# Raising the priority of the linear layers' matmuls, five of every six, in a three-block f32 model

## The chip, the cores and the metric

The kernel runs on one core of a Trainium2 chip. The metric is the device time of one execution in microseconds (us), and lower is better. Before the change it is 3328.61 us, the median of three runs (3328.02 to 3330.11).

## The reference

An activation of 512 tokens by 1024 channels passes through three residual blocks, all in float32. Each block projects its input with one wide matrix, feeds slices of the result to sequence mixers, projects the mixers' outputs, gates and sums them, and ends in a gated feed-forward network. The blocks differ in their mixers: a short convolution, pooling, a 31-tap convolution and differential attention in the first; a gated delta rule and an RWKV-7 scan in the second; gated linear attention and a state-space scan in the third. Of the second block, where most of what follows plays, the reference is:

```python
h = rms_norm_2(x, norm1_w[i]) * (1.0 + scale1) + shift1
p = h @ w_in[i]
qkv_a, z_a, b_a, a_a, p_b, gl_a, gl_b = split_cols(p, IN_SIZES)
y_a = gated_deltanet(qkv_a, z_a, b_a, a_a, conv_gdn[i], a_log[i], dt_bias[i], onorm_gdn[i])
y_b = rwkv7_time_mix(p_b, mu_rwkv[i], w0[i], w2[i], a0[i], a2[i], g2[i], k_k[i], k_a[i],
                     r_k[i], lnx_w[i], lnx_b[i])
y_a = y_a.astype(x.dtype) @ w_branch_gdn[i]
y_b = y_b.astype(x.dtype) @ w_branch_rwkv[i]
merged = jax.nn.sigmoid(gl_a) * y_a + jax.nn.sigmoid(gl_b) * y_b
x = x + gate1 * (merged @ w_out[i])
```

## The kernel before

Activations lie with channels on the 128 partitions and tokens along the free axis, so a 512 x 1024 activation is eight tiles of 128 x 512. Every linear layer keeps float32 precision by splitting both operands into a high part (float32r) and a remainder. One 128 x 128 weight block is then three matmuls over 512 tokens: high weight times high input, high weight times low input, low weight times high input. `lin` (line 358) makes one column of 128 output channels: it walks over the 8 (or 4, 11, 16) weight blocks along the contraction and accumulates 24 (or 12, 33, 48) matmuls into one PSUM bank of the pool `mm` (three banks). These are lines 368, 369 and 370. `product` (line 350, matmuls at lines 354 to 356) does the same on weights that were taken beforehand, for half columns and for the context of the third block. `tokens` (lines 404 to 406) is a third form, with the roles of weight and activation swapped.

Weights stream from HBM in pieces of eight blocks (`load`, line 315): one DMA, a copy on ScalarE that makes the high part (line 324) and a subtraction on VectorE that makes the low part (line 325).

The mixers issue many small matmuls of their own: transposes (line 655), block inversions (lines 707 and 714, inside `invert`), 64-row score blocks (line 1370), sums over the partitions in two halves (lines 616 and 617), state-space products (lines 2068 and 2082) and so on. Below they are called the mixers' matmuls, and those of lines 354 to 356, 368 to 370 and 404 to 406 the linear matmuls.

In the second block the mixers work head pair by head pair, j = 0 to 3. For each, `lins(j)` (line 1203) makes seven linear columns, then `rwkv` (line 1299, tiles tagged r, ra and fr) and `gdn` (line 1453, tiles tagged g, ga and fg) run side by side as generators, and their results are normalised and stored. `lins(j + 1)` and some gate columns (`aside`, 2, 1, 1 and 12 of them) follow in the text. After j = 3 the branch projection `w_branch_rwkv_2` reads the mixers' outputs, `yr`: its first three parts were stored earlier and are reloaded, its fourth is the last head pair's own result Y.

No order is written by hand. A scheduler takes the instructions as written, with their dependencies, and places on each engine, whenever that engine is free in its own estimate, the ready instruction of the highest priority; earlier in the text means higher priority. `first(n)` (line 252) raises what is inside by n places, 4000 by default, which is used on the weight pieces and on copies out of PSUM. The order that comes out is fixed in the program: at run time each engine issues its queue in order and waits at an instruction whose operands are not there yet. Linear columns written later than a mixer step thus serve as fill: they take the gaps while the mixer waits for VectorE or ScalarE.

Of the kernel before, what the change touches and what calls it, by code (L numbers as in the profile page):

```python
# [2 lines left out]

# [182 lines left out]
class K:  # L186
# [158 lines left out]
    def column(self, out, x):  # L345

        for a in range(0, P, 32):
            self.T.matmul(out[a:a + 32], lhsT=x[:, a:a + 32], rhs=self.ones[:, 0:1], start=True, stop=True)

    def product(self, ps, w, x, n=slice(0, S)):  # L350

        last = len(w) - 1
        for k, (wh, wl) in enumerate(w):
            self.T.matmul(ps[:, n], lhsT=wh, rhs=x[0][k][:, n], start=k == 0, stop=False)  # L354
            self.T.matmul(ps[:, n], lhsT=wh, rhs=x[1][k][:, n], start=False, stop=False)  # L355
            self.T.matmul(ps[:, n], lhsT=wl, rhs=x[0][k][:, n], start=False, stop=k == last)  # L356

    def lin(self, x, name, col, row=0, xc=None, n=S):

        self.tick()  # L360
        out = self.bank("mm")[:, :n]
        outc = self.bank("mm")[:, :256] if xc else None
        if xc is None:
            for k in range(len(x[0])):
                w = self.take([(name, row + P * k, col)])
                self.ahead()
                (wh, wl), last = w[0], len(x[0]) - 1
                self.T.matmul(out, lhsT=wh, rhs=x[0][k], start=k == 0, stop=False)  # L368
                self.T.matmul(out, lhsT=wh, rhs=x[1][k], start=False, stop=False)  # L369
                self.T.matmul(out, lhsT=wl, rhs=x[0][k], start=False, stop=k == last)  # L370
            return out
        w = self.take([(name, row + P * k, col) for k in range(len(x[0]))])
        self.product(outc, w, xc, slice(0, 256))
        self.product(out, w, x)
        self.ahead()
        return out, outc
# [1742 lines left out]
```

## Time and profile before

| | before |
|---|---|
| median of three runs | 3328.61 us |
| the profiled execution's own time | 3330.9 us |
| its span, first to last instruction | 3329.1 us |
| mean granted TensorE clock | 0.992 of full |
| TensorE (PE) busy | 3242.3 us, 97% |
| VectorE (DVE) busy | 2234.4 us, 67% |
| ScalarE (ACT) busy | 1497.2 us, 45% |
| the largest group of linear matmuls, line 368 on inputs h, 128 x 512 | 2400 recorded, 395 ns each as modelled |

Busy times are shares of the span. Matmuls are pipelined and the profile models their ends, so two that follow each other overlap in the records; what a matmul costs is read from one start to the next. An "x" after a row of the timeline counts merged records; a full-float32 matmul of the mixers leaves two records, a transpose one for each 128 x 128 block. In brackets stands the idle time of the engine ahead of the row, and what ended it.

### The profile page before, as it was taken

To read this page: it belongs to the slowest core of one execution; us is meant where nothing else is said; L and a number is where in the kernel's file an instruction comes from. 1 tells how busy PE (TensorE), PEld (TensorE's weight loads), DVE (VectorE), ACT (ScalarE), POOL (GpSimd) and SP (SyncE) were. 2 spreads that over 40 slices of the span, in tenths; PEclk is the share of its full clock that TensorE was granted. 3 is DMA by queue.
4 is the path that set the end of the run, shared out by engine and by line. 5 is a ranking of instruction groups with operands and counts; after the bars stand their busy time and mean duration, and the time that the engine had idled before them with its cause. 6 is when DMAs were issued, how large, how long until landed. Compare 5 with 4: busy or idle time off the path is not lost.

```text
span 3329.1 us, 48326 instructions
## 1 busy us (share of the span) xinstructions
PE 3242.3 (97%) x19041; PEld 2700.3 (81%) x19041; DVE 2234.4 (67%) x3675; ACT 1497.2 (45%) x2491; POOL 101.0 (3%) x186
## 2 busy tenths in 40 slices
PE   7999999999999999999999999999999999999998
PEld 6778888888887887887888887888877778888887
DVE  5696645986578577566887567777687996363344
ACT  6443433432346656654332334645546665232222
POOL 0000000000000000000000000000000001000000
PEclk9999999999999999999999999999999999999999
DMA  4223333665332112125367324222227567423332
GB/s 134 64 70 98 95 117 102 215 202 161 107 103 76 46 50 73 58 64 171 122 203 242 95 81 133 69 78 92 81 80 239 171 208 239 131 88 101 95 95 76
DMA packets 128324, 393.33 MB, mean 118 GB/s; under 512 B 16056, under 2 KB 23480, under 8 KB 128096
## 3 DMA queue, kind: packets, MB, share of 16 engines
q1 hardware_dynamic: 113776, 346.82, 33.6%
q0 software_dynamic: 13168, 42.36, 3.7%
q8 instruction: 150, 2.46, 0.3%
q10 hardware_dynamic: 1152, 1.05, 0.1%
q14 instruction: 78, 0.64, 0.1%
HBM read 358.44 MB, written 31.74 MB: 117 GB/s over the span
## 4 chain that ended last, share of the span: by engine, by line
PE 88%; DVE 6%; ACT 4%; issue 2%; DMA 1%; SPq 0%; POOL 0%; DVEq 0%; ACTq 0%; POOLq 0%
PE mm L368 20%; PE mm L369 20%; PE mm L370 20%; PE mm L354 3%; PE mm L355 3%; PE mm L356 3%; PE s L2082 1%; DVE wl L325 1%; PE s L2068 1%; ACT wh L324 1%; PE r L1370 1%; PE g L655 1%; PE mm L405 1%; PE r L655 1%; PE mm L406 1%
## 5 line engine op out<-in xcount | busy, mean ns | idle before, releaser
L368 PE MATMUL mm<-h,wh 128*128 128x512 f32 x2400 | 947.6, 395 | 1.8 <-ACT t L948 1.5
L369 PE MATMUL mm<-h,wh 128*128 128x512 f32 x2400 | 948.5, 395 | 0.0
L370 PE MATMUL mm<-h,wl 128*128 128x512 f32 x2400 | 947.3, 395 | 0.0
L324 ACT ACTIVATE wh<-wr 128x1024 fp32r<-128x1024 f32 x464 | 491.4, 1061 | 949.8 <-PE mm L369 663.5
L325 DVE TENSOR_TENSOR wl<-wr,wh 128x1024 fp32r<-128x1024 f32 x464 | 567.2, 1224 | 467.6 <-ACT wh L324 462.2
L368 PEld LDWEIGHTS mm<-h,wh 128*128 128x128 f32 x2400 | 452.7, 189 | 98.4 <-issue 5.5
L370 PEld LDWEIGHTS mm<-h,wl 128*128 128x128 f32 x2400 | 452.7, 189 | 96.9 <-issue 6.0
L369 PEld LDWEIGHTS mm<-h,wh 128*128 128x128 f32 x2400 | 452.8, 189 | 96.2 <-issue 5.4
L368 PE MATMUL mm<-p,wh 128*128 128x512 f32 x599 | 233.6, 390 | 0.0
L369 PE MATMUL mm<-p,wh 128*128 128x512 f32 x599 | 233.4, 390 | 0.1
L370 PE MATMUL mm<-p,wl 128*128 128x512 f32 x599 | 233.1, 389 | 0.0
L354 PE MATMUL mm<-h,wh 128*128 128x256 f32 (+1 forms) x480 | 159.5, 344 | 14.4 <-DVE t L1930 5.3
L355 PE MATMUL mm<-h,wh 128*128 128x256 f32 (+1 forms) x480 | 160.1, 339 | 1.1 <-DVE h L569 1.0
L356 PE MATMUL mm<-h,wl 128*128 128x256 f32 (+1 forms) x480 | 158.6, 335 | 0.0
L301 DVE SCALAR_TENSOR_TENSOR ac<-wa,adas,ac 128x1024 f32<-128x1024 f32 x98 | 125.5, 1282 | 23.9 <-DMA wa<-wa 23.5
L369 PEld LDWEIGHTS mm<-p,wh 128*128 128x128 f32 x599 | 112.4, 188 | 23.9 <-DVE p L430 0.8
L368 PEld LDWEIGHTS mm<-p,wh 128*128 128x128 f32 x599 | 112.4, 188 | 23.5
L370 PEld LDWEIGHTS mm<-p,wl 128*128 128x128 f32 x599 | 112.4, 188 | 23.4
L354 PEld LDWEIGHTS mm<-h,wh 128*128 128x128 f32 x480 | 92.4, 198 | 25.8 <-ACT h L568 4.6
L355 PEld LDWEIGHTS mm<-h,wh 128*128 128x128 f32 x480 | 94.3, 198 | 10.0 <-DVE h L569 2.0
L356 PEld LDWEIGHTS mm<-h,wl 128*128 128x128 f32 x480 | 94.6, 198 | 8.5
L750 DVE SCALAR_TENSOR_TENSOR f<-mm,par,f 128x511 f32<-128x511 f32 (+1 forms) x128 | 95.5, 746 | 1.1
(661 smaller groups left out, 5244.6 us busy)
## 6 DMA issues: line engine op xcount, KB each, us to landing
wr<-w SPq DMA_DIRECT2D x464, 512.0 KB, 3.7
wa<-wa SPq DMA_DIRECT2D x96, 512.0 KB, 4.3
e<-cum SPq DMA_DIRECT2D x64, 256.0 KB, 5.1
x<-x POOLq DMA_DIRECT2D x40, 256.0 KB, 4.5
s<-ecum SPq DMA_DIRECT2D x64, 128.0 KB, 4.8
cd<-t POOLq DMA_DIRECT2D x24, 256.0 KB, 2.3
gt<-t POOLq DMA_DIRECT2D x16, 256.0 KB, 2.5
fr<-gt SPq DMA_DIRECT2D x16, 256.0 KB, 3.0
```

The source lines that it names most:

```text
L301: self.V.scalar_tensor_tensor(a, raw, s[:, k, m:m + 1], a, op0=ALU.mult, op1=ALU.add)
L324: self.A.activation(hi, raw, AF.Copy)
L325: self.V.tensor_tensor(lo, raw, hi.bitcast(F32), op=ALU.subtract)
L354: self.T.matmul(ps[:, n], lhsT=wh, rhs=x[0][k][:, n], start=k == 0, stop=False)
L355: self.T.matmul(ps[:, n], lhsT=wh, rhs=x[1][k][:, n], start=False, stop=False)
L356: self.T.matmul(ps[:, n], lhsT=wl, rhs=x[0][k][:, n], start=False, stop=k == last)
L368: self.T.matmul(out, lhsT=wh, rhs=x[0][k], start=k == 0, stop=False)
L369: self.T.matmul(out, lhsT=wh, rhs=x[1][k], start=False, stop=False)
L370: self.T.matmul(out, lhsT=wl, rhs=x[0][k], start=False, stop=k == last)
L405: self.T.matmul(ps, lhsT=a, rhs=wl, start=False, stop=False)
L655: self.z.T.transpose(ps[:, c * P:(c + 1) * P], src[:, c * P:(c + 1) * P], self.z.ident)
L750: z.V.scalar_tensor_tensor(out[:, d:], src[:, :S - d], w[:, n - 1 - d:n - d], out[:, d:], op0=ALU.mult, op1=ALU.add)
```

## The change

In the two functions `product` and `lin` every matmul but one in six is put inside `self.first()`, so that its priority is 4000 places higher. Left as it was is the first matmul of weight blocks 0, 2, 4 and so on; the two that follow it on the same block, and all three of the next block, are raised. `tokens` is untouched, and so is everything that is computed.

```diff
+    def goes_on(self, k=1):
+
+        return self.first() if k % 2 else nullcontext()
+
     def product(self, ps, w, x, n=slice(0, S)):
 
         last = len(w) - 1
         for k, (wh, wl) in enumerate(w):
-            self.T.matmul(ps[:, n], lhsT=wh, rhs=x[0][k][:, n], start=k == 0, stop=False)
-            self.T.matmul(ps[:, n], lhsT=wh, rhs=x[1][k][:, n], start=False, stop=False)
-            self.T.matmul(ps[:, n], lhsT=wl, rhs=x[0][k][:, n], start=False, stop=k == last)
+            with self.goes_on(k):
+                self.T.matmul(ps[:, n], lhsT=wh, rhs=x[0][k][:, n], start=k == 0, stop=False)
+            with self.goes_on():
+                self.T.matmul(ps[:, n], lhsT=wh, rhs=x[1][k][:, n], start=False, stop=False)
+                self.T.matmul(ps[:, n], lhsT=wl, rhs=x[0][k][:, n], start=False, stop=k == last)
...
-                self.T.matmul(out, lhsT=wh, rhs=x[0][k], start=k == 0, stop=False)
-                self.T.matmul(out, lhsT=wh, rhs=x[1][k], start=False, stop=False)
-                self.T.matmul(out, lhsT=wl, rhs=x[0][k], start=False, stop=k == last)
+                with self.goes_on(k):
+                    self.T.matmul(out, lhsT=wh, rhs=x[0][k], start=k == 0, stop=False)
+                with self.goes_on():
+                    self.T.matmul(out, lhsT=wh, rhs=x[1][k], start=False, stop=False)
+                    self.T.matmul(out, lhsT=wl, rhs=x[0][k], start=False, stop=k == last)
```

In the changed program line numbers are higher by eight below these functions, and the three matmuls of `lin` stand at lines 375, 377 and 378, those of `product` at 359, 361 and 362. Counted over TensorE's whole queue, both programs have 16347 matmuls. The mixers' ones stand in 407 groups between linear matmuls before and in 308 groups after; groups that begin with a transpose at line 655 go from 63 to 33, with line 2082 from 33 to 23, with line 1005 from 21 to 12, with the sums of lines 616 and 617 from 69 to 52.

Three places show what moves. The first is TensorE's queue at the start of the second block's first head pair. The names g1411 and g1459 are banks of the gdn side (g1411 receives the transposed decay rows, line 1201), mm1446 and mm1688 are linear columns. Before:

```order
L368 MATMUL mm1446_8187<-h898_4694,wh1436_8112 128x512
L369 MATMUL mm1446_8187<-h899_4695,wh1436_8112 128x512
L370 MATMUL mm1446_8187<-h898_4694,wl1437_8113 128x512
L368 MATMUL mm1446_8187<-h900_4696,wh1436_8112 128x512
L655 MATMUL g1411_7960<-con2_64,ga1402_7921 128x128 x4
L369 MATMUL mm1446_8187<-h901_4697,wh1436_8112 128x512
```

After, in the changed program:

```order
L375 MATMUL mm1688_9076<-h898_4694,wh1442_8151 128x512
L377 MATMUL mm1688_9076<-h899_4695,wh1442_8151 128x512
L378 MATMUL mm1688_9076<-h898_4694,wl1443_8152 128x512
L663 MATMUL g1411_7960<-con2_64,ga1402_7921 128x128 x4
L624 MATMUL g1459_8236<-ga1457_8234,bd64r4_66 128x512
L625 MATMUL g1459_8236<-ga1458_8235,bd64r4_66 128x512
L375 MATMUL mm1688_9076<-h900_4696,wh1442_8151 128x512
```

The transposes into g1411 stood inside column mm1446, 13 matmuls into it; now they stand in the next column, 12 matmuls into mm1688, which is 23 linear matmuls later.

The second place is TensorE's queue in the last head pair, j = 3, where `rwkv` goes from its bonus sum (bank r2332, lines 616 and 617) to its first scores (bank r2349, line 1370). mm2573 is a gate column; mm2617 and mm2626 are columns of the branch projection behind the mixers. Before, the end of that stretch:

```order
L370 MATMUL mm2573_12806<-h894_4690,wl2566_12742 128x512
L368 MATMUL mm2573_12806<-h896_4692,wh2565_12741 128x512
L369 MATMUL mm2573_12806<-h897_4693,wh2565_12741 128x512
L1370 MATMUL r2349_11872<-ra2296_11681,ra2315_11740 128x128 x4
L1370 MATMUL r2361_11905<-ra2296_11681,ra2315_11740 128x128 x4
L370 MATMUL mm2573_12806<-h896_4692,wl2566_12742 128x512
```

After, the whole of it:

```order
L377 MATMUL mm2626_13029<-fg2598_12951,wh2590_12911 128x512
L378 MATMUL mm2626_13029<-fg2597_12950,wl2591_12912 128x512
L624 MATMUL r2332_11796<-ra2330_11794,bd64r4_66 128x512
L625 MATMUL r2332_11796<-ra2331_11795,bd64r4_66 128x512
L1378 MATMUL r2349_11872<-ra2296_11681,ra2315_11740 128x128
L663 MATMUL g2344_11841<-con2_64,ga2342_11837 128x128 x4
L663 MATMUL g2345_11853<-con2_64,fg2278_11566 128x128 x4
L663 MATMUL g2348_11861<-con2_64,fg2284_11605 128x128 x4
L1378 MATMUL r2349_11872<-ra2296_11681,ra2315_11740 128x128 x3
```

Before, 28 linear matmuls stood between the second half of the sum and the scores; now none does, since all gate columns and what the branch projection can do without Y stand ahead of the sum.

The third place is the end of that head pair: the sums of Y's two normalisations (banks r2523 and r2531) and the branch projection's first matmuls on Y. Before, from the end of the last gate column mm2588:

```order
L616 MATMUL r2531_12520<-ra2529_12518,bd64r4_66 128x512
L370 MATMUL mm2588_12908<-h906_4702,wl2581_12844 128x512
L368 MATMUL mm2617_12989<-fg2594_12944,wh2585_12877 128x512
L617 MATMUL r2531_12520<-ra2530_12519,bd64r4_66 128x512
L369 MATMUL mm2617_12989<-fg2595_12945,wh2585_12877 128x512
L370 MATMUL mm2617_12989<-fg2594_12944,wl2586_12878 128x512
```

After:

```order
L1455 MATMUL r2520_12494<-fr2257_11425,ra2515_12478 128x128 x3
L624 MATMUL r2523_12501<-ra2521_12499,bd64r4_66 128x512
L625 MATMUL r2523_12501<-ra2522_12500,bd64r4_66 128x512
L624 MATMUL r2531_12520<-ra2529_12518,bd64r4_66 128x512
L625 MATMUL r2531_12520<-ra2530_12519,bd64r4_66 128x512
L375 MATMUL mm2617_12989<-ra2602_12960,wh2585_12877 128x512
L377 MATMUL mm2617_12989<-ra2603_12961,wh2585_12877 128x512
```

From the second half of r2332's sum to the first matmul on Y the queue held 143 linear matmuls before and holds 9 after; the other 134 stand ahead of that sum.

## Rows read from the trace of the kernel before

**Rows 1.** The page: the busy time of the engines, and the chain that ended last by engine.

```profile
PE 3242.3 (97%) x19041; PEld 2700.3 (81%) x19041; DVE 2234.4 (67%) x3675; ACT 1497.2 (45%) x2491; POOL 101.0 (3%) x186
...
PE 88%; DVE 6%; ACT 4%; issue 2%; DMA 1%; SPq 0%; POOL 0%; DVEq 0%; ACTq 0%; POOLq 0%
```

**Rows 2.** The timeline of TensorE in a linear column of the second block. The first two rows are five linear matmuls apart; the third is one half of a sum between two linear matmuls. Columns: start, length, engine, line, operation, output and inputs, shape, count.

```profile
1299.95 0.40 PE L368 MATMUL mm<-h,wh 128*128 128x512 f32 x1
...
1301.09 0.39 PE L370 MATMUL mm<-h,wl 128*128 128x512 f32 x1
...
1302.91 0.41 PE L616 MATMUL r<-ra,bd64r 128*128 128x512 f32 x1
1303.16 0.39 PE L369 MATMUL mm<-h,wh 128*128 128x512 f32 x1
```

**Rows 3.** The same view at two other interruptions of linear columns: a pair of transposes in the second block, with a run of five transposes further on, and line 2082 (128 x 64 weights) in the third block, there also in a long run.

```profile
1458.60 0.48 PE L369 MATMUL mm<-h,wh 128*128 128x512 f32 x1
1458.91 0.41 PE L655 MATMUL g<-con,mga 128*128 128x128 f32 x2
1459.08 0.48 PE L370 MATMUL mm<-h,wl 128*128 128x512 f32 x1
1459.39 0.61 PE L707 MATMUL r<-ra,mra 128*128 128x128 f32 x4
...
1471.11 0.71 PE L655 MATMUL g<-con,ga 128*128 128x128 f32 x5
1471.66 0.61 PE L707 MATMUL r<-ra,mra 128*128 128x128 f32 x4
...
2565.70 0.48 PE L370 MATMUL mm<-h,wl 128*128 128x512 f32 x1
2566.11 0.43 PE L2082 MATMUL s<-e,g 128*64 128x128 f32 x2
2566.47 0.50 PE L368 MATMUL mm<-h,wh 128*128 128x512 f32 x1
2566.81 0.39 PE L369 MATMUL mm<-h,wh 128*128 128x512 f32 x1
...
2571.01 1.74 PE L2082 MATMUL s<-e,g 128*64 128x128 f32 x26
2572.68 0.87 PE L2006 MATMUL s<-con,xs 128*128 128x128 f32 x6
```

**Rows 4.** What TensorE waited for from 1000 to 1530 us, the second block's mixers: engine, output, line and releaser, total us, times, longest us.

```profile
PE g L655 <- ACT ga L1198: 3.9, 1, 3.9
PE g L1478 <- DVE fg L1230: 3.2, 3, 1.3
...
PE r L616 <- ACT ra L1289: 2.2, 3, 1.1
```

**Rows 5.** Stretches from 1000 to 1530 us in which the clock was granted at half: the stretch and its length, then busy time and count of PE, PEld, DVE, ACT and POOL, then the granted clock, the DMA share and GB/s.

```profile
1008.90:1012.30 3.40, 3.20 (x10) 2.71 (x11) 3.12 (x5) 2.83 (x6) 0.00 (x0) 0.50 0.75 167
1145.50:1148.80 3.30, 3.30 (x9) 2.62 (x9) 1.42 (x3) 1.17 (x1) 1.08 (x2) 0.50 0.58 209
1159.10:1162.40 3.30, 3.30 (x12) 2.59 (x11) 2.44 (x7) 1.08 (x2) 0.00 (x0) 0.50 0.00 0
1275.20:1278.50 3.30, 3.07 (x9) 1.89 (x7) 3.30 (x5) 3.25 (x5) 0.54 (x1) 0.50 0.05 21
1520.90:1524.30 3.40, 3.40 (x9) 2.67 (x8) 3.21 (x6) 2.04 (x3) 0.00 (x0) 0.50 0.56 183
```

**Rows 6.** TensorE's timeline at the end of one of the waits at line 1478.

```profile
1157.63 1.16 PE L1478 MATMUL g<-fg 64*128 64x128 f32 x8 [1.25 <-DVE fg L1230]
```

**Rows 7.** Five stretches of the last head pair, from the bonus sum to the first matmul on Y, columns as in rows 5.

```profile
1422.60:1429.20 6.60, 6.31 (x29) 4.89 (x27) 6.57 (x12) 3.03 (x6) 0.37 (x1) 1.00 0.08 29
1429.20:1444.70 15.50, 15.48 (x97) 12.63 (x97) 13.51 (x27) 8.54 (x20) 0.71 (x2) 1.00 0.36 118
1444.70:1491.20 46.50, 46.42 (x392) 42.48 (x391) 25.32 (x59) 25.28 (x64) 0.54 (x1) 1.00 0.08 24
1491.20:1507.30 16.10, 16.10 (x118) 14.04 (x118) 9.46 (x18) 7.91 (x10) 0.54 (x1) 1.00 0.18 45
1507.30:1519.80 12.50, 9.39 (x41) 7.14 (x39) 5.99 (x8) 7.77 (x10) 0.54 (x1) 1.00 0.33 112
```

**Rows 8.** The same five stretches, counting only instructions that write or read a bank `mm`, so that the first column (PE) counts the linear matmuls. The further columns are PEld, DVE and ACT.

```profile
1422.60:1429.20 6.60, 6.31 (x28) 4.88 (x26) 0.00 (x0) 0.58 (x1) 1.00 0.08 29
1429.20:1444.70 15.50, 9.11 (x33) 5.82 (x33) 0.00 (x0) 0.58 (x1) 1.00 0.36 118
1444.70:1491.20 46.50, 8.98 (x22) 3.79 (x22) 0.00 (x0) 0.58 (x1) 1.00 0.08 24
1491.20:1507.30 16.10, 6.18 (x23) 4.21 (x24) 0.00 (x0) 0.60 (x1) 1.00 0.18 45
1507.30:1519.80 12.50, 9.12 (x38) 6.92 (x37) 0.00 (x0) 0.58 (x1) 1.00 0.33 112
```

**Rows 9.** The timeline of VectorE from the bonus sum (first row) to the last operand of the first scores (second row), and that of TensorE at the first matmul on Y.

```profile
1422.59 0.69 DVE L1342 TENSOR_TENSOR ra<-r,fr 128x512 f32<-128x512 f32 x1 [1.50 <-PE r L617]
...
1428.46 0.68 DVE L1352 TENSOR_TENSOR ra<-ra,ra 128x512 f32<-128x512 f32 x1
...
1519.85 0.96 PE L368 MATMUL mm<-ra,wh 128*128 128x512 f32 x3 [3.16 <-ACT ra L429]
```

More of the change, by code (lines that the diff above doesn't have):

```diff
@@ L1 @@
 import numpy as np
-from contextlib import ExitStack, contextmanager
+from contextlib import ExitStack, contextmanager, nullcontext
 import concourse.bass as bass
```

## The prediction

> **What bounds the kernel now.** I read the page first, then TensorE's timeline in dense stretches, then TensorE's waits, and last the windows of the second block's last head pair. The page shows TensorE busy for 97% of the span and holding 88% of the chain that ended last [rows 1]: the kernel is one queue of matmuls, and almost nothing else is ever late. The change adds no matmul and takes none away, so it can move the time in three ways only: the price of going from linear matmuls to the mixers' and back, the time in which TensorE stands and waits, and the clock it is granted.
>
> A linear matmul costs 0.228 us from start to start: five of them lie between 1299.95 and 1301.09 [rows 2]. All fill below is counted by that number.
>
> **Part 1, fewer interruptions.** The queue loses 99 of its 407 groups of mixers' matmuls between linear ones. What does an interruption cost beyond its own work? For the halves of sums, nothing much: the one at 1302.91 takes 0.25 us [rows 2]. For a pair of transposes: from 1458.60 to 1459.39 there are two linear matmuls (0.456) and two transposes, which in a run cost (1471.66 - 1471.11) / 5 = 0.11 each [rows 3]; 0.79 - 0.456 - 0.22 leaves 0.11. For a pair of line 2082: from 2565.70 to 2566.81 are 1.11 us; less 0.456 for two linear matmuls, and less two records at (2572.68 - 2571.01) / 26 = 0.064, it leaves 0.53 [rows 3]. So of the 99, the 10 groups of line 2082 give 10 x 0.5 = 5.0 us and the 30 that begin with a transpose 30 x 0.11 = 3.3. The rest, half sums and full-size matmuls among them, I put at the half sums' nothing. Term: -8.3 us. Bounds: 0 (the merged groups win nothing, if small waits made up the 0.11) and 5.0 + 89 x 0.11 = 14.8.
>
> The Trainium skill, "TensorEngine Tiling (Array Packing)", section Tiling Modes, says that changing the tiling mode drains TensorE. The 128 x 64 matmuls of line 2082 fit that, with 0.53 us a visit; the pair of transposes, full-size, does not pay that much. By that rule alone only groups with partial tiles would gain, and this part would come to the 5.0 us.
>
> **Part 2, waits that go.** In the second block's mixers TensorE now waits 3.9 us for the transposed decay rows (line 655 behind line 1198), 3.2 us in three waits at line 1478, and 2.2 us in three at line 616 [rows 4]. The new queue puts more fill ahead of them. The rows' transposes come 23 linear matmuls later, 5.2 us against a wait of 3.9. The waits at line 1478 are at most 1.3 each, and each now has a column or more of extra fill ahead of it (a column is 24 x 0.228 = 5.5 us). The clock counts too: the half-clock stretch of 1159.10 begins 1.5 us after a wait at line 1478 ended at 1157.63, and that of 1520.90 some 1.1 us after the wait that ended at 1519.85 [rows 5, 6, 9]. The first of rows 5 lies at the rows' transposes, the second and fourth near waits at line 616. At half clock 3.4 us do the work of 1.7, so each costs 1.7. Gone: 3.9 + 1.7 for the rows, 3.2 + 1.7 for line 1478. For line 616 (2.2 us and two stretches, 3.4) I take half, 2.8, since about as many linear matmuls stand behind the sum before it as now. Term: -13.3 us. Bounds: 0 and 3.9 + 3.2 + 2.2 + 4 x 1.7 = 16.1.
>
> **Part 3, the fill that is used up early.** This is the part that decides. Raised matmuls overtake the mixers' steps, so the last head pair reaches its bonus sum with its fill already spent: of 143 linear matmuls between that sum and the first matmul on Y (144 in the windows, one lies on an edge [rows 8]), 134 stand ahead of the sum afterwards. They cost 134 x 0.228 = 30.6 us there, in place of here. The question is how much shorter the 97.2 us of the five stretches [rows 7] become without them.
> - First stretch, 6.6 us with 28 of them [rows 7, 8]. VectorE is busy in nearly all of it, 6.57 us, from the bonus at 1422.59 to the last operand, which starts at 1428.46 [rows 7, 9]. It stays 6.6, and TensorE stands still in it.
> - Second, 15.5 us with 33, of which 9 stay. At most 24 x 0.228 = 5.5 shorter, 10.0; VectorE has 13.5 us of work here [rows 7], of which its weight splits move away with the fill. I take 12.0.
> - Third, 46.5 us with 22 (5.0 us), the inversions. Lower bound 41.5. Each step of an inversion waits for a copy or a subtraction, and the linear matmuls stand in just those gaps. I take 46.
> - Fourth, 16.1 us with 23 (5.2 us). Lower bound 10.9. A chain of short steps between TensorE and VectorE; I take 14.5.
> - Fifth, 12.5 us with 38. A pure chain through the other engines, for whose end TensorE waits 3.16 us even with the fill [rows 9]. I take 12.0; lower bound 11.0, if the weight pieces' work on ScalarE was in its way.
>
> Sum 91.1 in place of 97.2, so 6.1 us of the 30.6 come back. Term: +24.5 us. Bounds: with every stretch at its lowest (6.6 + 10.0 + 41.5 + 10.9 + 11.0 = 80.0) it is 30.6 - 17.2 = +13.4; with none shorter, +30.6. Behind a standstill as long as the first stretch the clock will fall as it did behind the 3.16 us [rows 5, 9]: one more half-clock stretch, +1.7, bounds 0 and 3 x 1.7 = 5.1. Queued behind the waiting scores stand the gdn side's transposes; since the stretch is counted whole, their delay is in it.
>
> **Part 4, new short waits.** In the middle head pairs some inversion steps lose the linear matmuls that stood between them. No row prices that: at one or two linear matmuls each, some ten of them make 3 us; bounds 0 and 6. In the first and third blocks the order lets linear matmuls run ahead of the mixers by at most 25 and is level again when each stage ends; I count nothing.
>
> **The sum.** 24.5 + 1.7 + 3.0 - 13.3 - 8.3 = +7.6 us. Against the profiled execution's own 3330.9 us (its span 3329.1, and 1.8 around it) that is 3338.5; that execution lies 2.3 us over the median of the runs shown, 3328.6, so against the median it is 3336.2. I forecast 3336 us, 0.2% slower.
>
> **The rivals.**
> - *Faster: interruptions are dear everywhere.* Place: all 99 groups that go. Price: if each were worth 0.3 us, between the transposes' 0.11 and line 2082's 0.53, part 1 would be -30, and the sum 24.5 + 1.7 + 3.0 - 13.3 - 30 = -14, that is 3315. It outweighs the rest from 0.16 us a group and shows as faster from 0.23. For it: line 2082. Against it: the half sum that costs nothing, and that only 10 of the 99 are of line 2082. Chance 0.12.
> - *No change: the mixers of the last head pair were held up by the fill.* Then the third and fourth stretches fall near their lower bounds, the five sum to 83, and part 3 is +16.4; the sum is -0.5 and the time 3328. For it: TensorE's 46.42 busy of 46.5 us in the third stretch [rows 7]. Against it: VectorE and ScalarE are each busy for over half of that stretch and hand on to each other. Chance 0.33, for all that ends within 6.7 us.
> - *Much slower: nothing comes back and the clock stays low.* The naked stretches cost the full 30.6 with three half-clock stretches, and line 616 goes on waiting: 30.6 + 5.1 + 3.0 - 10.5 - 8.3 = +20, that is 3349. For it: the clock fell after a wait as short as 1.25 us [rows 5, 6]. Chance 0.10.
> - *Nothing moves.* The rows of the order exclude it.
>
> **How the numbers follow.** About 0.2% of the time, 6.7 us, is what a measurement of this kernel can tell from no change. My forecast and its neighbours on the slow side beyond that have 0.45, the much slower case 0.10, no change 0.33, faster 0.12: faster 0.12, same 0.33, slower 0.55. My likeliest case alone runs from 3330 to 3344; for 8 in 10 the range reaches over no change and into both outer cases, 3321 to 3351.
>
> **What would show it.** In the profile of the changed kernel TensorE should wait some 6 us for the first scores of the last head pair (line 1378, behind VectorE) and 6 to 10 us in two or three waits on the way to the first matmul on Y, with the linear matmuls solid ahead of the bonus sum. The long wait at line 663 and those at line 1486 should be gone, and two half-clock stretches with them. In the state-space stage line 2090 should come in fewer visits. I am wrong if TensorE's waits in the second block's mixers do not grow over the 3.9 + 3.2 + 2.2 + 3.2 = 12.5 us of now [rows 4, 9]. If the span falls although they grow, the price of an interruption is what I mis-sized.

## The result, and the profile after

The changed kernel takes 3355.46 us (median of 4 runs, 3353.24 to 3358.86); the kernel before, on the same chip, 3329.36 (4 runs, 3328.02 to 3330.94). The ratio is 1.0081, with a 95% interval of 1.0066 to 1.0096: 26 us slower. The forecast of 3336 had the direction, but 7.6 us instead of 26, and the time lies outside the range of 3321 to 3351. The profiled execution took 3358.86 us, with a span of 3357.1.

Line numbers have grown by 8 in most of the program: 655 is now 663, 1370 is 1378, 1478 is 1486, 616 is 624, 2082 is 2090; the three matmuls 368 to 370 of a linear column are 375, 377 and 378.

The page of the changed kernel, the two lines that answer to [rows 1]:

```profile
PE 3245.4 (97%) x19041; PEld 2710.8 (81%) x19041; DVE 2238.0 (67%) x3675; ACT 1497.7 (45%) x2493; POOL 101.6 (3%) x186
...
PE 87%; DVE 5%; ACT 5%; issue 2%; DMA 1%; SPq 0%; POOL 0%; DVEq 0%; ACTq 0%; POOLq 0%
```

The page hides the loss: shares and counts are nearly as before. The waits of TensorE from 1000 to 1560 us, the second block's mixers, answer to [rows 4] (engine, output, line and releaser; total us, times, longest):

```profile
PE r L1378 <- DVE ra L1363: 7.7, 1, 7.7
PE mm L375 <- ACT ra L437: 7.2, 1, 7.2
PE r L624 <- ACT ra L1297: 4.5, 3, 2.1
PE g L663 <- ACT ga L1206: 2.1, 1, 2.1
PE r L663 <- ACT mra L703: 2.0, 2, 1.2
PE g L1546 <- DVE ga L1541: 1.3, 1, 1.3
PE r L1449 <- DVE ra L1444: 1.2, 1, 1.2
PE g L663 <- ACT mga L703: 1.0, 1, 1.0
PE g L1486 <- DVE fg L1238: 0.9, 2, 0.6
```

The first scores of the last head pair (line 1378) and the first matmul on Y (line 375) now wait over 7 us each. Of the waits that were to go, line 1486 fell from 3.2 to 0.9 us and the decay rows (line 663 behind 1206) only from 3.9 to 2.1; those at line 663 behind 703, a step of the inversions, and at line 1546, a step from one chunk's state to the next, are new.

The last head pair from the bonus sum to the first matmul on Y, as in [rows 7] with the fourth and fifth stretch in one (stretch and length; busy time and count of PE, PEld, DVE, ACT, POOL; granted clock, DMA share, GB/s):

```profile
1451.60:1459.30 7.70, 0.02 (x1) 0.00 (x0) 7.60 (x16) 2.61 (x5) 0.00 (x0) 0.65 0.00 0
1459.30:1476.20 16.90, 15.83 (x73) 13.41 (x73) 9.45 (x19) 6.77 (x17) 0.00 (x0) 0.66 0.05 16
1476.20:1519.90 43.70, 42.88 (x371) 39.04 (x371) 24.47 (x59) 23.23 (x61) 0.00 (x0) 1.00 0.03 7
1519.90:1546.30 26.40, 14.08 (x97) 10.90 (x96) 12.98 (x25) 10.01 (x14) 0.00 (x0) 0.74 0.07 21
```

The second stretch has 73 matmuls where it had 97, and yet takes 16.9 us where it took 15.5. The reason stands in the clock. Two stretches at half clock (1.2 GHz) lie here, in place of the single one of 3.4 us at 1520.90 [rows 5]:

```profile
1453.90:1471.00 17.10, 11.68 (x45) 9.93 (x46) 11.78 (x26) 5.91 (x13) 0.00 (x0) 0.50 0.05 16
1532.40:1549.50 17.10, 6.38 (x13) 3.43 (x12) 9.12 (x14) 7.99 (x12) 0.00 (x0) 0.50 0.10 27
```

Both traces, cut at the same matmuls, give an account of the whole. "Standing" is the time between the end of one matmul record and the start of the next; "half clock" is half of the matmul time in half-clock stretches; "work" is what remains. The same kernel was profiled once more later (run e9_changed, span 3351.9), and the table takes that profile minus the one of before, in us:

| stretch of before | span | standing | half clock | work |
|---|---|---|---|---|
| 0 to 867, first block | +0.7 | +3.0 | 0 | -2.3 |
| 867 to 1421.5, mixers up to the last bonus sum | +24.2 | +0.3 | -3.4 | +27.3 |
| 1421.5 to 1601, last head pair and branch | -1.3 | +18.3 | +7.3 | -26.9 |
| 1601 to 3329, the rest | -0.8 | +3.4 | -1.6 | -2.7 |
| all | +22.8 | +25.1 | +2.2 | -4.6 |

The +27.3 and -26.9 are for the most part one thing. The cut is a matmul of line 1486 (1494 in the changed kernel) beside the bonus sum; ahead of it stand 129 more linear matmuls than before, 129 x 0.228 = 29.4 us of work that moved across it. (At the bonus sum's second half, a few matmuls on, it is the 134 of the prediction.) The rest, -2.1 ahead of the cut and +2.5 behind it, is what became of the mixers' own matmuls: +0.4 together. The profile of before took 3330.9 us, 1.6 over the median of its runs, and e9_changed's 0.5 less than its median, so the +22.8 is some 2 to 3 us short of the difference of the medians. The first profile has the same two middle rows to 0.1 us; it has 6.7 us more half clock elsewhere, such as a stretch of 3.4 us at 272.9 that the second does not have.

### The profile page after: what moved, and what is told of

It reads as the page before. It is cut to its first block, busy times and chain, and to the rows that moved or that the text cites. A ratio compares the mean times of both kernels' runs of the same rounds, so it can differ in the third digit from the quotient of the medians.

```text
span 3357.1 us, 48284 instructions
## 1 busy us (share of the span) xinstructions
PE 3245.4 (97%) x19041; PEld 2710.8 (81%) x19041; DVE 2238.0 (67%) x3675; ACT 1497.7 (45%) x2493; POOL 101.6 (3%) x186
## 4 chain that ended last, share of the span: by engine, by line
PE 87%; DVE 5%; ACT 5%; issue 2%; DMA 1%; SPq 0%; POOL 0%; DVEq 0%; ACTq 0%; POOLq 0%
PE mm L375 20%; PE mm L377 20%; PE mm L378 20%; PE mm L359 3%; PE mm L361 3%; PE mm L362 3%; ACT wh L324 1%; PE s L2090 1%; DVE wl L325 1%; PE r L1378 1%; PE s L2076 1%; PE mm L414 1%; PE mm L413 1%; PE mm L412 1%; PE g L663 1%
## 5 line engine op out<-in xcount | busy, mean ns | idle before, releaser
L378 PE MATMUL mm<-h,wl 128*128 128x512 f32 x2400 | 937.4, 391 | 0.0
L301 DVE SCALAR_TENSOR_TENSOR ac<-wa,adas,ac 128x1024 f32<-128x1024 f32 x98 | 125.3, 1280 | 26.9 <-DMA wa<-wa 26.4
L377 PEld LDWEIGHTS mm<-p,wh 128*128 128x128 f32 x599 | 112.6, 188 | 26.1 <-DVE p L438 2.9
L2069 ACT ACTIVATE e<-e,tok 128x128 f32<-128x128 f32 x256 | 82.1, 393 | 35.1 <-DMA e<-cum 20.4
```

The costliest lines, as they stand in the source:

```text
L301: self.V.scalar_tensor_tensor(a, raw, s[:, k, m:m + 1], a, op0=ALU.mult, op1=ALU.add)
L2069: A.activation(m[:, n], m[:, n], AF.Relu, scale=-1.0, bias=tok[:, i, 64 + r:65 + r])
```

## The experiments

Theory F: the second block's mixers spend their fill (the linear matmuls) early, and the standstills and the low clock at the last head pair are the loss. Its rivals stand with each run. The first five kernels have a switch in place of the change's `self.first()`:

```diff
+    lift = HP
...
-        return self.first() if k % 2 else nullcontext()
+        return self.first(self.lift) if self.lift and k % 2 else nullcontext()
```

**Where it happens.** e1_outside sets the switch to 0 inside `second`; in e2_inside the two values are exchanged, and the class begins with `lift = 0`:

```diff
 def second(z, h):
+    z.lift = 0
...
+    z.lift = HP
     return m
```

> The raise is kept in the first and third blocks and taken out of the second block's mixers; 35 of the 99 groups of mixers' matmuls that the change removes stay removed. Theory F (the loss sits in the second block's mixers: fill spent early, then standstills and a low clock behind them): the +26 us fall to the +3.5 of the first block's new wait and about +1 in the third, so 3331 to 3335 us, with no half-clock stretch longer than 6.8 us. Rival S (each raised column costs a little wherever it stands): the linear matmuls outside these mixers are more than four fifths of all, so some +21 us stay, 3350.

> The reverse: the raise only in the second block's mixers, 64 of the 99 groups removed. Theory F: +20 to +25 us, 3350 to 3354, with about 30 us of TensorE standing still between 1000 and 1560 us and the two half-clock stretches of 17.1 us in place. Rival S: +4 to +6, 3334.

e1_outside took 3330.70 us against 3327.58 before, ratio 1.0009 (1.0000 to 1.0018), just under theory F's range; e2_inside 3352.01, ratio 1.0074 (1.0057 to 1.0091). So +3.1 and +24.4, 27.5 for the two where the whole is 26.1: theory F holds and rival S falls. e1_outside shows the old waits again in the mixers, among them:

```profile
PE g L664 <- ACT ga L1208: 3.9, 1, 3.9
PE g L1489 <- DVE fg L1240: 3.2, 3, 1.3
PE mm L376 <- ACT ra L438: 3.1, 1, 3.1
```

The +3.1 outside is not free of cause either. In the changed kernel a raised matmul of the first block stands in the queue ahead of its operand's split, and a gate's matmul in the third block waits until ScalarE has read its bank; the kernel before has neither wait, e1_outside has both:

```profile
271.31 0.50 PE L377 MATMUL mm<-p,wh 128*128 128x512 f32 x1 [2.19 <-DVE p L438]
...
2115.50 0.49 PE L1705 MATMUL a<-lo,lw 96*128 96x512 f32 x1 [2.87 <-ACT y L1706]
```

**How much fill goes early.** Three kernels between and beyond, in the order of the edits: e3_threes leaves the first matmul of every block unraised (the edit stands in `product` and in `lin`), e7_gates_only the next head pair's columns in the second block, and e4_columns raises all but the first matmul of a column (its expectation says "first block", but that block's second and third matmul are raised too).

```diff
-            with self.goes_on(k):
+            with nullcontext():
```

```diff
+                z.lift = 0
                 now = lins(j + 1)
+                z.lift = HP
```

```diff
-        return self.first(self.lift) if self.lift and k % 2 else nullcontext()
+        return self.first(self.lift) if self.lift and k else nullcontext()
```

> The first matmul of every block is left unraised, so that three come together and not six; 55 of the 99 groups go, and the queue of the last head pair's bonus sum has 50 linear matmuls more ahead of it than before the change, in place of 119. Theory F with a loss in proportion to the fill that is ahead: 26 x 50/119 = +11, 3338 to 3342 us. Rival E (what counts is only that the fill is spent before the last head pair ends, which it is here too, 74 matmuls early in its middle): most of the loss stays, 3347 to 3355. If the clock is the larger part, the long half-clock stretches are gone and the time is under 3338.

> The changed kernel without the raise in the columns of the next head pair in the second block's mixers; the gates' columns there stay raised. 68 of the 99 groups go, but only 47 linear matmuls more stand ahead of the last head pair's bonus sum, in place of 119. Theory F (the fill spent early sets the loss): as with three at a time (50 ahead, +15): +12 to +16 with the +3 of the other blocks, 3339 to 3344 us. Rival G (the loss follows the raised columns or the groups that go, 68 of 99): +18 or more, 3346 us.

> All but the first block of a column is raised, so that nearly whole columns come together: 192 of the 407 groups go, and up to 242 linear matmuls stand earlier in the second block's mixers, 214 in the first block's attention, 99 in the third block. Theory F: further +10 to +25 us beside the +26, 3365 to 3380, since more of the mixers' steps are left bare and the clock falls more often, and 192 groups give back only about 0.06 us each, 11 us. Rival I (interruptions are dear and the loss is only the last head pair, whose fill can be spent no more than once): under the 3355 of the change, 3340 to 3350.

| kernel | linear matmuls more ahead of the last bonus sum | groups gone | us | ratio, 95% interval | against before |
|---|---|---|---|---|---|
| e1_outside | 0 | 35 | 3330.70 | 1.0009 (1.0000 to 1.0018) | +3.1 |
| e7_gates_only | 62 | 68 | 3344.80 | 1.0051 (1.0036 to 1.0066) | +16.9 |
| e3_threes | 59 | 55 | 3342.92 | 1.0042 (1.0027 to 1.0057) | +15.3 |
| the change | 134 | 99 | 3355.46 | 1.0081 (1.0066 to 1.0096) | +26.1 |
| e4_columns | 134 | 192 | 3432.74 | 1.0308 (1.0293 to 1.0324) | +105.2 |

The second column is counted in the traces' order of matmuls, at the second half of the bonus sum. The 50, 47 and 119 of the expectations are the counts at the sum before it, which lies at 1401 us in the kernel before; the forecast in proportion changes little, 26 x 59/134 = 11.5.

From 0 to 134 the loss grows with the fill that is ahead, but not in proportion. The first 60 matmuls cost more than forecast: e3_threes, at 3342.92, and e7_gates_only, at 3344.80, both missed theory F's ranges (up to 3342 and 3344) by a little, and e7_gates_only lies between its two theories. The wait at the first matmul on Y grows from 3.2 us to the full 7.2 in both, with one half-clock stretch of 17.1 us each.

And e4_columns fell far beyond both theories, with no more fill ahead of the last bonus sum than the change, since there is no more to move: 9 are left between that sum and the first matmul on Y in both. At the bonus sums of the second and third head pair it has 172 and 177 more ahead, where the change has 112 and 111. Its waits from 1000 to 1640 us show that the naked steps are no longer only those of the last head pair:

```profile
PE r L1379 <- DVE ra L1361: 12.5, 3, 6.6
PE r L625 <- ACT ra L1298: 9.4, 5, 2.3
PE mm L376 <- ACT ra L438: 7.2, 1, 7.2
```

Line 1379, the first scores, waits in three of the four head pairs (4.1, 1.8 and 6.6 us). I had priced e4_columns as if the fill could only be missed at the last one. Nor is the loss all in the second block: by the same account its profile has +75.5 us from 867 to 1601, +33.3 behind (standing +34.4, half clock +13.5, work -14.6), and -8.2 in the first block.

**What an interruption costs.** e6_price is the kernel before with a measuring stretch behind the second block's mixers:

```diff
...
+        line = lambda: T.matmul(wide, lhsT=z.bd64r, rhs=y, start=True, stop=True)
+        part64 = lambda: T.matmul(thin[:64, :P], lhsT=x[:, :64], rhs=x[:, :P], start=True, stop=True)
+        turn = lambda: T.transpose(thin[:, :P], x[:, :P], z.ident)
+            for f in (part64, turn):
+                some(40, line)
+                some(40, f)
+                for _ in range(20):
+                    some(2, line)
+                    some(2, f)
...
```

> The kernel before with a measuring stretch behind the second block's mixers, all operands ready: 40 linear matmuls, 40 matmuls with 128 x 64 weights, then the two kinds by twos 20 times; the same with transposes. What the mixed order takes over the two grouped runs, by 20, is the price of an interruption alone. Theory D (as the prediction has it): 0.53 us for a pair with 128 x 64 weights, so that 20 visits take 10.6 us more than grouped, and 0.11 for a pair of transposes, 2.2 us more. Rival N (what the trace showed at such pairs was mostly a wait for an operand, since the 35 groups that went outside the second block gave back 5 us and the 64 within it nothing): under 0.1 us a visit for both, 0 to 2 us.

TensorE's timeline there, in the one execution of this kernel (start, length, line, operation, shape, count; a matmul of plain f32 leaves two records, so four are two matmuls):

```profile
1559.26 9.38 PE L1283 MATMUL r<-h,bd64r 128*128 128x512 f32 x40
1568.57 8.95 PE L1284 MATMUL g<-h 128*64 128x128 f32 x80
1577.45 0.73 PE L1283 MATMUL r<-h,bd64r 128*128 128x512 f32 x2
1578.11 0.65 PE L1284 MATMUL g<-h 128*64 128x128 f32 x4
1578.69 0.73 PE L1283 MATMUL r<-h,bd64r 128*128 128x512 f32 x2
...
1602.31 9.36 PE L1283 MATMUL r<-h,bd64r 128*128 128x512 f32 x40
1611.52 2.67 PE L1285 MATMUL g<-con,h 128*128 128x128 f32 x23
...
1615.80 0.71 PE L1283 MATMUL r<-h,bd64r 128*128 128x512 f32 x2
...
1629.53 0.71 PE L1283 MATMUL r<-h,bd64r 128*128 128x512 f32 x2
```

With 128 x 64 weights the 20 mixed rounds run from 1577.45 to 1602.31, 1.243 us each. Grouped, two of each take 2 x 9.31 / 40 + 2 x 8.88 / 40 = 0.910 (starts from 1559.26 to 1568.57 to 1577.45). A visit costs 0.33 us. With transposes the rounds take (1629.53 - 1615.80) / 20 = 0.687, against 2 x 9.21 / 40 + 2 x 4.28 / 40 = 0.675 grouped: 0.01 us. So each theory was nearly right for one kind: the partial tiles have a price, two thirds of mine, and the transposes have none. The kernel before agrees: its nine visits of one matmul of line 2082 between linear ones take 0.564 us by the median, 0.34 over 2 x 0.111, and one to four transposes of line 1021 there take 0.117, 0.225, 0.340 and 0.445. Nor does it come from plain f32 alone: of line 2036, plain f32 at full size, two records between linear matmuls take 0.866 us, and four in the changed kernel (line 2044) 1.727, twice as much, so that the visit itself adds nothing.

The Trainium skill, "TensorEngine Tiling (Array Packing)", section Tiling Modes, says that changing the tiling mode drains TensorE, and the trace agrees: the full-size transposes pay nothing, the 64-column tiles 0.33 us for a change there and back.

Then why did the state-space stage gain so little? In the stretch from 2484 to 2941 us e1_outside has 1.3 us less work, not 5. The order of the instructions answers that: line 2082 is entered from linear matmuls 23 times and not 33, but from the stage's full-size mixer matmuls 20 times and not 13. In all its runs fall from 46 to 43. Three changes fewer, at 0.33, are 1.0 us.

The first block does not follow that count. Counted in the traces, TensorE changes its tile size 83 times there before and 87 times after, and yet the work falls by 2.3 us, with 15 groups gone. In e3_threes it is 83 changes, 7 groups gone and 1.1 us; in e4_columns 85 changes, 37 groups gone and 6.9 us. So a group that went was worth 0.15 to 0.19 us there, whatever its tile size; what makes it so, no run isolates.

**What the clock costs.** e5_cover is the changed kernel with extra matmuls in the two long standstills; e9_cover repeats it, e9_cover_all fills two shorter waits as well (the 6 and 9 of the edit, which the others lack), and e9_changed is the changed kernel once more, all three on one chip.

```diff
+    def idle(self, ps, x, n):
+        for _ in range(n):
+            self.T.matmul(ps, lhsT=self.bd64r, rhs=x, start=True, stop=True)
...
+        if j == 3 and not Lt:
+            z.idle(ps, gh, 33)
         rows = slice(64 * e, 64 * e + 64)
...
+            if j == 3:
+                z.idle(cr.bank(), gh, 6)
             V.scalar_tensor_tensor(Y, cr.total(Y, z.bd64r), -1.0 / 64, Y, op0=mult, op1=add)
+            if j == 3:
+                z.idle(cr.bank(), gh, 9)
...
+            if j == 3:
+                z.idle(cr.bank(), gh, 31)
             V.scalar_tensor_tensor(Yg, Yg, z.q("onorm_2"), rn[0], op0=mult, op1=mult)
```

> The changed kernel with 64 extra linear matmuls whose results are overwritten or unused: 33 in front of the first scores of the last head pair (7.7 us of standstill there) and 31 behind the totals of Y, where TensorE waits 7.2 us. They add 64 x 0.228 = 14.6 us of work, all of it where TensorE stood still. Theory C (the low clock behind the standstills is paid extra, 5.9 + 3.8 us of the two stretches of 17.1 us): both stretches go, the time falls by 6 to 10 us to 3346 to 3350. Rival W (only the waiting counts, and the clock would have fallen anyway): no gain, 3355, or up to 3358 with the few matmuls that spill over. In the mixers the waits at these two places are under 1 us in either case.

> The changed kernel as it is, for a comparison with the two covered kernels on one chip: 3353 to 3357 us by either theory.

> The kernel with 64 extra matmuls of the run before, again, since its interval overlapped that of the changed kernel. Theory C: 5 to 7 us under the changed kernel on the same chip. Rival W: within 2 us of it.

> The same with 15 more extra matmuls, 6 and 9, in the two waits of 1.4 and 2.1 us ahead of the last totals, where the kernel with 64 still had a half-clock stretch of 10.2 us. Theory C: that stretch goes too (about 5 us of its length were work, so 2 to 3 us less), 7 to 10 us under the changed kernel, although 79 x 0.228 = 18 us of work were added. Rival W: not under the changed kernel by more than 2.

e5_cover took 3349.17 us, ratio 1.0065 (1.0049 to 1.0082). On one chip, where the kernel before took 3329.01: e9_changed 3354.09, ratio 1.0082 (1.0068 to 1.0096); e9_cover 3349.95, 1.0069 (1.0057 to 1.0082); e9_cover_all 3348.85, 1.0065 (1.0053 to 1.0078). Adding 18 us of useless work made the kernel 5.2 us faster by the medians, under the 7 to 10 forecast, and the 64 of e9_cover 4.1, under 5 to 7. The intervals against the kernel before overlap, but the runs themselves lie apart: 3353.56 to 3355.76 for e9_changed, 3348.51 to 3352.31 for e9_cover, 3346.85 to 3350.91 for e9_cover_all. The traces say where it comes from. From 1421.5 to 1601 the changed kernel's two profiles are 1.3 us shorter than before, e5_cover and e9_cover 4.9 and 5.4, e9_cover_all 6.9. e9_cover_all from the bonus sum to the first matmul on Y:

```profile
1448.90:1456.50 7.60, 7.24 (x32) 5.64 (x31) 7.57 (x17) 2.62 (x5) 0.00 (x0) 1.00 0.00 0
1456.50:1468.70 12.20, 10.89 (x74) 8.98 (x74) 9.08 (x19) 6.58 (x17) 0.00 (x0) 1.00 0.07 21
1468.70:1512.40 43.70, 42.89 (x371) 39.05 (x371) 24.47 (x59) 23.21 (x61) 0.00 (x0) 1.00 0.03 7
1512.40:1538.60 26.20, 22.31 (x140) 18.36 (x139) 12.95 (x24) 10.00 (x14) 0.00 (x0) 1.00 0.07 21
```

The clock is granted in full throughout, and the second stretch falls from 16.9 to 12.2 us. By the account of 1421.5 to 1601, the half clock goes from +7.3 to -1.7 against before (9.0 us), standing from +18.3 to +2.9, and work from -26.9 to -8.1. So 18.8 us of work were laid over 15.4 us of standing; 3.4 spilled over, and 9.0 - 3.4 = 5.6 us were gained. Theory C holds for the clock; what I had left out of its forecast is the spill.

**An attempt to beat both kernels.** e8_before_cover fills three waits of the kernel before:

```diff
+        z.idle(c.bank(), gh, 17)
         tok = ch(c.transposes(rows, z.tile("q")))
...
+            if j == 3:
+                z.idle(cr.bank(), gh, 14)
...
+            z.idle(c.bank(256), ctx[7], 10, z.ident)
             hc += z.rms(c, ctx, z.mod[:, 56:64], z.mod[:, 48:56], 256, hcs)
```

> The kernel before, without any raise, with extra matmuls whose results nobody uses where TensorE stands still longest: 17 linear ones at the transposes of the decay rows (wait of 3.9 us at 1005 us), 14 behind the totals of Y (3.2 us at 1517), and ten products with the identity, 256 columns wide, ahead of the column sums of the third block's context norm (4.4 us at 2016). Each wait is followed by a half-clock stretch, of 3.4, 3.4 and 6.8 us. Theory C (a covered standstill keeps the clock up): 1.7 + 1.7 + 3.4 = 6.8 us less, 3319 to 3324, and the three stretches are gone. Rival W (the clock falls for another reason): 3327 to 3330, the stretches stay or move.

It took 3338.61 us, ratio 1.0033 (1.0021 to 1.0045): 12.2 us slower by the medians, outside the ranges of both theories. Against the profile of before, which is 4.5 us over the median on this chip, the span grew by 5.7: the half-clock loss fell by 4.3 us over the span (20.3 to 16.0) and the standing by 3.8, but 13.8 us of work were added. Only the 14 at Y fell into their hole; with the first 17 TensorE still waits 2.4 us for the rows. The third cover shows the mistake:

```profile
2018.33 6.27 PE L348 MATMUL a<-a,con 128*128 128x256 f32 x20 [2.94 <-DMA a<-ctx]
```

It waits 2.9 us for the context itself and then runs for 6.3, longer than the 4.4 us that it was to fill. No kernel here beats the one of before. A part of one does: e4_columns reached the first block's end at 858.7 us, where the kernel before was at 866.8, since work fell by 6.9 us there and standing by 1.2. No run raised whole columns in the first block alone.

## Why the prediction was wrong

By its own terms, against the account of the second profile (+22.8):

- **Part 1, fewer interruptions: -8.3 predicted, -4.6 measured.** The failed step is "the 10 groups of line 2082 give 10 x 0.5 = 5.0 us and the 30 that begin with a transpose 30 x 0.11 = 3.3". The transposes give 0.01 each (e6_price); the 0.11 was read from a pair behind which line 707 follows, and the late start there, 0.31 us behind the linear matmul instead of 0.228 [rows 3], belongs to the next group. The 64 groups that go in the second block's mixers give nothing on balance (work +27.3 - 26.9 = +0.4 there, with the moved fill in both). A visit of line 2082 is worth 0.33, and only 3 of the 10 are saved, because I counted groups between linear matmuls and not changes of tile size. What was saved, 2.3 us in the first block and 2.7 behind 1601 us, lies largely where I had counted nothing: 0.15 to 0.19 us a group in the first block, near the 0.16 of the rival "interruptions are dear everywhere", which did not hold in the second.
- **Parts 2 and 4 in the mixers up to the last bonus sum: -10.3 predicted (-13.3 + 3), -3.1 measured.** The clock gave back two thirds of the forecast (-5.1 predicted, -3.4 measured). The waits fell short of it: "Gone: 3.9 + 1.7 for the rows" failed, since 2.1 of the 3.9 us stayed, and the inversions and solves ahead of the bonus sum lost more fill than "some ten of them make 3 us" allowed: waits of 6.1 us there are new. Standing came out level (+0.3) where -5.2 was in the sum.
- **Part 3, the fill used up early: +24.5 + 1.7 = +26.2 predicted, +18.3 + 7.3 = +25.6 measured.** This was the part that decides, and that its sum holds is luck, for its split does not. "One more half-clock stretch, +1.7" was mis-sized, and its bound of 5.1 too low: two stretches of 17.1 us came, 9.0 us of loss against 1.7 before. The standstills were put too long: the four stretches of the changed kernel take 94.7 us, of which 7.4 are half clock, so 87.3 at full clock where 91.1 was predicted (e9_cover_all took 89.7, with the spill in it); the third took 43.7 for 46. The two errors cancel. Reckoned by these stretches, as the prediction does, the part comes to 30.6 - (97.2 - 94.7) = +28.1; the account has the difference, 2.5, in its work behind the cut.
- **Part 4, first and third blocks: "I count nothing" failed.** Standing grew by 3.0 us in the first block and 3.4 behind the second's mixers, with -1.6 of half clock: +4.8. A queue that is level again at a stage's end may still have put a matmul ahead of its operand within it. e1_outside has the net, +3.1, in its median.

The sum: 7.6 + 3.7 + 7.2 - 0.6 + 4.8 = 22.7. The first profile, with 28.0, has 6.7 of half clock more outside the mixers, less 1.5 of other differences. Of the signs to look for, the wait at the first scores (7.7, "some 6") and the growth of the waits came as said; the way to the first matmul on Y has 11.9 us in four waits and not 6 to 10 in two or three, and the waits at lines 663 and 1486 shrank and did not go. The rival nearest to the truth was the much slower one, 3349 with a chance of 0.10. Its clock, 5.1, was nearer to the 7.3 that came, but by no means all the fill was lost, and the missing gains of parts 1 and 2 made up the rest.

## What to carry to other kernels

Independent matmuls that fill a chain's gaps are a stock: before they are given priority, count how many are left at each step that needs them, the last above all, and price the standstill there together with the clock behind it. Grouping like matmuls is worth only what a change costs: measure it by mixing and grouping the same instructions, count changes of tile size beside changes of purpose, and do not carry a price from one stage to the next, since here the first block, the second and the state-space stage each paid differently. A gain from a wait that goes belongs into the sum only after looking at what else waits at that place once the fill stands ahead of it.

## What the runs showed of the hardware

One stretch at half clock began 2.3 us into a standstill of 7.7 us and lasted 17.1 us, although TensorE was busy for 11.7 of them; in the kernel before, no stretch inside the mixers was longer than 3.4. Useless matmuls in the standstill kept it at full.

Plain f32 matmuls with 128 x 64 weights take 8.88 / 80 = 0.111 us a record when all write to the same 64 partitions (e6_price), and 0.064 in line 2082's long run [rows 3], where they write to the two halves in turn. That fits the Trainium skill, "TensorEngine Tiling (Array Packing)", section Tiling Modes, by which separate tiles work at the same time; no run here changed that alone.
